# A fourth pair of row blocks in Strassen's form, in another order, in a two-layer encoder trunk

## Chip, cores and metric

One core of a Trainium2 chip runs the whole program. Time is device microseconds of that core; the figure is the median of several runs. The engines are named as the profile names them: PE (matmul; PEld is its weight load), DVE (VectorE), ACT (ScalarE), POOL (GpSimd), SP (which issues the weights' DMAs).

## The reference, cut to what matters

256 rows, width 2048, two layers, everything in float32:

```
for l in range(2):
    u = rmsnorm(x) ;  proj = u @ w_in[l]                  # latents, q/k/v, gate_a, gate_b (2048 wide each)
    y_a = mla_attention(...) @ w_o_mla[l] ;  y_b = neighbourhood_attention(...) @ w_o_na[l]
    merged = sigmoid(gate_a) * y_a + sigmoid(gate_b) * y_b
    x = x + merged @ w_out[l]
    x = x + square(relu(rmsnorm(x) @ w_ff1[l])) @ w_ff2[l]
return rmsnorm(x)
```

The change concerns the gate products (`u @` the last 4096 columns of `w_in`) and, through a shared table, `merged @ w_out`.

## The kernel before

Each float32 operand is split into a rounded high part and the low part that is left (`hi`, `lo` for weights; a `pair` holds both for an activation). A product is three matmuls: high by high, low activation by high weight, high activation by low weight. For a weight tile ACT casts the high part (L177 in `gemm_s`, L201 elsewhere) and DVE subtracts to get the low part (L178, L202).

`gemm_s` computes a product of all 256 rows with 1024 columns. It takes the 2048 rows of the weight in eight "row pairs" j of 256 rows, 1 MB each, in the sequence of a table `order`. A row pair is a 2 by 2 block product. In the plain form it has 8 block products, 24 matmuls of 512 columns; if j is in the table `pairs` it is done by a Strassen (Winograd) form with 7 products, 21 matmuls. The Strassen form needs sums: of the activation blocks, made once by DVE (L364 to L367, `sums_of`) and split by `forms` (ACT L375, DVE L376); and of the weight blocks, made for every call by DVE (L465 of 1024 columns, L468 and L469 of 512). So its weights are split from seven quarter tiles in place of four. All products of a call accumulate in eight banks of PSUM; in the end they are combined (ACT copies bank 1, L477; DVE adds, L476).

Two kinds of call concern us:

- *Gate calls*, four in each layer (`gemm_s(wi, C_GB..., ORDER, MIXED)`, then twice `C_GA`). Between the first and second stand two plain products with `w_o_na`. Their part buffers `hi` and `lo` are four each, of 1024 columns, and the sums have two buffers of 1024, one row pair's worth. The first call of a layer starts while the latents' norms (PE L329 and L298, DVE L332, L305, POOL L307, DVE L294), the rotary key (DVE L710, PE L528, DVE L530 to L532) and `forms` are still at work.
- *Output projection calls*, two in each layer (`gemm_s(w_out[l], ..., ORDER, MERGED)`). There tiles are "strips" of up to 2048 columns, three buffers each for `hi` and `lo`, and one buffer of sums.

The feed-forward calls use tables of their own (`FIRST`, `SECOND`, order 0 to 7). Tiles of 512 columns (pairs, results, forms) come from a pool of `NSLOT` slots. POOL issues the accumulating DMAs of the feed-forward (L870) and those of the bias tables; their descriptors lie in a scratch area. Weights come by SP into three `raw` buffers.

The code is recorded by a framework that orders the instructions of each engine by a timeline of its own, and gives a tile whichever buffer of its pool comes free first. Each engine then runs its instructions strictly in that order, and waits for what an instruction needs.

```
first = next(j for j in order if j in pairs)
for j in order:
    ...                       # DMA of row pair j
    if j not in pairs:  ...   # plain: cut(raw), 8 products
    if j == first: drain()    # all side work that still waits is recorded here
```

Of the kernel before, what the change touches and what calls it, by code (L numbers as in the profile page):

```python
# [58 lines left out]

NSLOT, SMALL, RBUFS, HBUFS = 52, 8, 3, 4


FIRST, SECOND = (3, 5), (2, 4, 6)


MIXED, MERGED = (1, 2, 3), (1, 2, 3)
ORDER = [0, 4, 1, 5, 2, 6, 3, 7]


SPACING, LAG1, LAG2 = 6, 13, 3
# [3 lines left out]
def trunk(ctx: ExitStack, tc: tile.TileContext, x, w_in, w_uq, w_ukv, rpb, w_o_mla, w_o_na,  # L76
# [303 lines left out]
    def blocks(acts, sums, pairs):  # L380

        def get(j):
            a = [have(acts, 2 * j + i) for i in range(2)]
            hi, lo = ([x[:, o + t * P:o + (t + 1) * P] for x in a for t in range(2)] for o in (0, S))
            if j in pairs:
                for v, x in zip((hi, lo), have(sums, j)):
                    v += [x[:, i * P:(i + 1) * P] for i in range(4)]
            return hi, lo
        return get
# [268 lines left out]
    for l in range(DEPTH):  # L658
# [57 lines left out]
        def gate(th, g):  # L716
            def evac(r):
                for i in range(2):
                    for t in range(2):
                        nc.scalar.activation(r[t, i], r[t, i], AF.Tanh, scale=mix.half[:, t:t + 1])  # L720
                        th[t, 2 * g + i] = r[t, i]
            return evac

        def local(c4):
            def merge(t, ps):
                m = part[t, c4]
                nc.vector.scalar_tensor_tensor(m, m, 1.0, ps, op0=ALU.add, op1=ALU.mult)

            gemm_a(w_o_na[l], c4 * 512, att_na, merge)

        mixed = blocks(xg, xs4, MIXED)
        gemm_s(wi, C_GB, mixed, ORDER, MIXED, gate(part, 0))
        local(0)
        local(1)
        gemm_s(wi, C_GB + 1024, mixed, ORDER, MIXED, gate(part, 1))
        for g in range(2):
            gemm_s(wi, C_GA + g * 1024, mixed, ORDER, MIXED, gate(other, g))

# [80 lines left out]
        for g in range(2):  # L819
# [10 lines left out]

            gemm_s(w_out[l], g * 1024, blocks(mg, ms4, MERGED), ORDER, MERGED, residual)
        mlp.scale()
# [126 lines left out]
```

## Time and profile before

| what | value |
|---|---|
| median of 3 runs | 2631.06 us (2629.96 to 2631.34) |
| profiled execution | 2630.92 us, span 2629.1 us |
| PE busy / DVE busy / ACT busy | 2599.1 / 2116.7 / 1457.8 us |
| granted TensorE clock | 0.998 |
| gate calls of layer 0 | 215.7 to 259.2, 281.8 to 323.3, 323.3 to 364.8, 364.8 to 406.3 us |
| output projection of layer 0 | starts at 539.4 us |

Rows of the trace read: start us, duration us, engine, line, operation, output<-inputs, shape, count, and in brackets how long the engine was idle before and what ended that. Rows of a window give for each engine the busy time in it and the count of instructions, then the granted clock, the share of the DMA engines and GB/s. Rows of waits read: who waited, for whom, us in total, times, longest. The duration of a row is longer than the distance to the next one where instructions overlap.

### The profile page before, as it was taken

Reading aid. Unit: us, or ns where it says so; the run is one execution under the profiler, and the core shown is the slowest. Engines: PE = TensorE matmul, PEld = TensorE weight load, DVE = VectorE, ACT = ScalarE, POOL = GpSimd, SP = SyncE. Lnnn points to the kernel's source line nnn. Section 1 sums busy time; section 2 is a strip of 40 time slices with the busy share of each in tenths; the row PEclk is TensorE's granted clock in tenths of the full one; section 3 lists DMA queues with packets and bytes.
Section 4 is the critical chain, followed back from the end, with each engine's and each line's share of the span. In section 5 each row is a group of like instructions: output and inputs, shape, how many; then the busy total and the mean of one; then the engine's idle time right before and its main releaser. Section 6 shows DMA issues by size and latency. Waiting matters only on the chain.

```text
span 2629.1 us, 32272 instructions
## 1 busy us (share of the span) xinstructions
PE 2599.1 (99%) x12498; PEld 2183.3 (83%) x12498; DVE 2116.7 (81%) x2496; ACT 1457.8 (55%) x1719; POOL 97.2 (4%) x117
## 2 busy tenths in 40 slices
PE   8999999999999999999999999999999999999998
PEld 7888888878888888888888888888788888888886
DVE  6678789789888888888667787896998888888885
ACT  6555556546655545546545555564566555455553
POOL 1100000000000010000001000000000000100000
PEclk9999999999999999999999999999999999999999
DMA  7555555555567485675565555644555765756744
GB/s 243 182 159 192 192 195 170 162 179 192 200 198 242 160 244 199 199 241 178 190 195 174 173 180 190 207 146 160 188 196 192 217 210 195 244 196 198 259 160 148
DMA packets 175258, 508.97 MB, mean 194 GB/s; under 512 B 13696, under 2 KB 18176, under 8 KB 175104
## 3 DMA queue, kind: packets, MB, share of 16 engines
q1 hardware_dynamic: 166192, 490.08, 55.7%
q0 software_dynamic: 8768, 16.78, 3.3%
q8 instruction: 98, 1.61, 0.2%
q14 instruction: 56, 0.46, 0.1%
q10 hardware_dynamic: 144, 0.04, 0.0%
HBM read 492.18 MB, written 2.10 MB: 188 GB/s over the span
## 4 chain that ended last, share of the span: by engine, by line
PE 76%; issue 19%; DVE 2%; ACT 1%; POOL 1%; DMA 0%; SPq 0%; POOLq 0%; DVEq 0%; ACTq 0%
PE bank L428 47%; PE bank L244 8%; PE bank L279 7%; PE bank L248 4%; PE bank L283 3%; PE bank L223 1%; PE bank L398 1%; DVE lo L178 1%; PE bank L252 1%; PE bank L224 1%; PE bank L254 1%; PE bank L253 1%; POOL xt L870 1%; PE bank L558 0%; ACT hi L177 0%
## 5 line engine op out<-in xcount | busy, mean ns | idle before, releaser
L428 PE MATMUL bank<-hi,pair 128*128 128x512 f32 x5156 | 1269.8, 390 | 7.0 <-ACT hi L177 6.2
L428 PEld LDWEIGHTS bank<-hi,pair 128*128 128x128 f32 x5156 | 964.9, 188 | 210.6 <-ACT hi L177 9.9
L177 ACT CAST hi<-raw 128x2048 fp32r<-128x2048 f32 (+3 forms) x416 | 630.0, 1534 | 449.1 <-PE bank L428 323.0
L178 DVE TENSOR_TENSOR lo<-raw,hi 128x2048 fp32r<-128x2048 f32 (+3 forms) x416 | 751.0, 1817 | 94.7 <-ACT hi L177 61.5
L428 PE MATMUL bank<-lo,pair 128*128 128x512 f32 x2578 | 677.4, 389 | 0.0
L428 PEld LDWEIGHTS bank<-lo,pair 128*128 128x128 f32 x2578 | 483.7, 188 | 100.2
L178 DVE TENSOR_TENSOR lo<-sums,hi 128x2048 fp32r<-128x2048 f32 (+1 forms) x134 | 254.6, 1909 | 176.3 <-ACT hi L177 118.5
L177 ACT CAST hi<-sums 128x2048 fp32r<-128x2048 f32 (+1 forms) x134 | 214.8, 1603 | 290.3 <-DVE sums L469 187.4
L202 DVE TENSOR_TENSOR lo<-raw,hi 128x1024 fp32r<-128x1024 f32 (+1 forms) x224 | 268.7, 1205 | 121.9 <-ACT hi L201 114.2
L201 ACT CAST hi<-raw 128x1024 fp32r<-128x1024 f32 (+1 forms) x224 | 230.0, 1036 | 208.6 <-PE bank L279 84.8
L244 PE MATMUL bank<-hi,pair 128*128 128x512 f32 x1024 | 259.6, 390 | 0.0
L244 PEld LDWEIGHTS bank<-hi,pair 128*128 128x128 f32 x1024 | 190.6, 188 | 38.9
L476 DVE TENSOR_TENSOR wide<-wide,bank 128x512 f32<-128x512 f32 x336 | 216.1, 680 | 4.5 <-PE bank L428 4.1
L279 PE MATMUL bank<-pair,hi 128*128 128x512 f32 x768 | 203.2, 397 | 4.5 <-ACT hi L201 3.2
L279 PEld LDWEIGHTS bank<-pair,hi 128*128 128x128 f32 x768 | 136.3, 190 | 26.9 <-ACT hi L201 3.6
L248 PE MATMUL bank<-lo,pair 128*128 128x512 f32 x512 | 142.8, 392 | 0.0
L465 DVE TENSOR_TENSOR sums<-raw 128x1024 f32<-128x1024 f32 x110 | 134.1, 1219 | 5.7 <-DMA raw<-in_w_ff 5.1
L283 PEld LDWEIGHTS bank<-pair,lo 128*128 128x128 f32 x768 | 106.9, 190 | 8.7
L283 PE MATMUL bank<-pair,lo 128*128 128x256 f32 x768 | 111.6, 283 | 0.0
L248 PEld LDWEIGHTS bank<-lo,pair 128*128 128x128 f32 x512 | 95.2, 188 | 18.9
L408 DVE TENSOR_TENSOR pair<-wide,pair 128x512 fp32r<-128x512 f32 x108 | 72.4, 686 | 13.9 <-ACT pair L407 13.9
L870 POOL DMA_DIRECT2D xt<-wide x48 | 42.3, 968 | 977.0 <-DVE wide L476 702.6
(131 smaller groups left out, 1727.8 us busy)
## 6 DMA issues: line engine op xcount, KB each, us to landing
raw<-in_w_ff SPq DMA_DIRECT2D x256, 1024.0 KB, 5.2
raw<-in_w_in SPq DMA_DIRECT2D x124, 1024.0 KB, 5.1
raw<-in_w_out SPq DMA_DIRECT2D x32, 1024.0 KB, 5.3
raw<-in_w_o_na SPq DMA_DIRECT2D x16, 1024.0 KB, 5.0
raw<-in_w_o_mla SPq DMA_DIRECT2D x16, 1024.0 KB, 5.0
xt<-wide POOLq DMA_DIRECT2D x48, 256.0 KB, 6.8
raw<-in_w_ukv SPq DMA_DIRECT2D x8, 1024.0 KB, 5.6
raw<-in_w_uq SPq DMA_DIRECT2D x8, 768.0 KB, 4.6
```

Of the source, the lines that this page charges most:

```text
L177: nc.scalar.copy(hi, src)
L178: nc.vector.tensor_tensor(lo, src, hi.bitcast(F32), op=ALU.subtract)
L201: nc.scalar.copy(hi, src)
L202: nc.vector.tensor_tensor(lo, src, hi.bitcast(F32), op=ALU.subtract)
L244: nc.tensor.matmul(ps[t], a, wh[:, k], start=k0 + k + i == 0, stop=False)
L248: nc.tensor.matmul(ps[t], sides(have(acts, k0 + k), t)[0], wl[:, k], start=False, stop=k0 + k == nk - 1)
L279: nc.tensor.matmul(ps[m], wh[:, k, m * P:(m + 1) * P], have(acts, k0 + k), start=k0 + k == 0, stop=False)
L283: nc.tensor.matmul(ps[m][:, :S], wl[:, k, m * P:(m + 1) * P], have(acts, k0 + k)[:, :S], start=False, stop=k0 + k == nk - 1)
L408: nc.vector.tensor_tensor(lw, src, h.bitcast(F32), op=ALU.subtract)
L428: nc.tensor.matmul(b[i], x, y, start=count[i] == 1, stop=count[i] == total[i])
L465: nc.vector.tensor_tensor(ts[0].rearrange("p (a n) -> p a n", a=2), raw[:, :512].rearrange("p (a n) -> p a n", a=1).to_broadcast([P, 2, 512]),
L476: add = lambda o, a, c: nc.vector.tensor_tensor(o, a, c, op=ALU.add)
```

## The change

```diff
-NSLOT, SMALL, RBUFS, HBUFS = 52, 8, 3, 4
+NSLOT, SMALL, RBUFS, HBUFS = 54, 8, 3, 4
...
-MIXED, MERGED = (1, 2, 3), (1, 2, 3)
-ORDER = [0, 4, 1, 5, 2, 6, 3, 7]
+MIXED, MERGED = (0, 1, 2, 3), (1, 2, 3)
+ORDER = [4, 5, 0, 1, 6, 2, 3, 7]
...
-    nc = bacc.Bacc(..., dynamic_dma_scratch_size=8192)
+    nc = bacc.Bacc(..., dynamic_dma_scratch_size=4096)
```

In the gate calls row pair 0 is done in Strassen's form too: the order was plain 0, plain 4, Strassen 1, plain 5, Strassen 2, plain 6, Strassen 3, plain 7, and is plain 4, plain 5, Strassen 0, Strassen 1, plain 6, Strassen 2, Strassen 3, plain 7. In the output projection 0 stays plain: plain 4, plain 5, plain 0, Strassen 1, plain 6, Strassen 2, Strassen 3, plain 7. The activations of pair 0 are formed once in each layer (two tiles more, hence the slots), and its activation blocks are scaled by ACT into a tile first (L501) before they are split. The halved scratch makes room for the slots. The number of DMAs is the same.

What that does to the engines' orders shows in three places. First, PE in the first gate call of layer 0, from the end of the two plain pairs; before:

```order
345 L428 MATMUL bank<-lo,pair 128x512 x8
346 L428 MATMUL bank<-hi,pair 128x512 x4
347 L428 MATMUL bank<-lo,pair 128x512 x2
348 L428 MATMUL bank<-hi,pair 128x512 x2
349 L528 MATMUL bank<-small,turn 128x256
350 L329 MATMUL bank<-ones,acc 128x2 x2
351 L428 MATMUL bank<-hi,pair 128x512 x6
352 L428 MATMUL bank<-lo,pair 128x512
353 L428 MATMUL bank<-hi,pair 128x512 x10
354 L428 MATMUL bank<-lo,pair 128x512 x4
355 L298 MATMUL bank<-diag,ones 128x128
```

and now:

```order
343 L428 MATMUL bank<-lo,pair 128x512 x8
344 L428 MATMUL bank<-hi,pair 128x512 x4
345 L428 MATMUL bank<-lo,pair 128x512 x2
346 L428 MATMUL bank<-hi,pair 128x512 x4
347 L428 MATMUL bank<-lo,pair 128x512 x2
348 L528 MATMUL bank<-small,turn 128x256
349 L329 MATMUL bank<-ones,acc 128x2 x2
350 L298 MATMUL bank<-diag,ones 128x128
351 L428 MATMUL bank<-hi,pair 128x512 x6
```

Of the matmuls ahead of L528, two high ones and a low one now belong to Strassen pair 1, not to pair 0, and the norm's L298 follows L329 with no product between them. The same stretch on DVE, now (numbers count the tiles; 2312 and 2377 are the raw weights of pairs 0 and 1):

```order
L178 TENSOR_TENSOR lo_2349<-sums_2332,hi_2348 128x1024
L323 TENSOR_TENSOR acc_2141<-acc_2141,small_2173 128x256
L260 TENSOR_TENSOR small_2225<-bank_2176,small_2223 128x256
L465 TENSOR_TENSOR sums_2379<-raw_2377 128x1024
L178 TENSOR_TENSOR lo_2385<-raw_2377,hi_2384 128x1024
L710 TENSOR_TENSOR small_2225<-small_2225,rrow_419 128x256
L468 TENSOR_TENSOR sums_2380<-raw_2377,sums_2379 128x512
L469 TENSOR_TENSOR sums_2380<-raw_2377,sums_2380 128x512
L530 TENSOR_TENSOR small_2294<-bank_2292,sin_sb_83 128x256
```

Pair 1's sums and first low part (`lo_2385`, which PE wants ahead of L528) now stand between the last part of pair 0 and the rotary key's L710, which L528 needs.

Second, ACT at the end of the third gate call; before (3277 and 3278 are the sums of pair 3, 3319 is plain pair 7):

```order
L177 CAST hi_3290<-sums_3277 128x1024
L177 CAST hi_3294<-sums_3278 128x1024
L177 CAST hi_3321<-raw_3319 128x1024
L177 CAST hi_3325<-raw_3319 128x1024
L477 COPY wide_3353<-bank_3138 128x512
```

and now (3319 and 3320 are pair 3's sums, 3361 is plain pair 7):

```order
L177 CAST hi_3332<-sums_3319 128x1024
L477 COPY wide_3395<-bank_3170 128x512
L177 CAST hi_3336<-sums_3320 128x1024
L177 CAST hi_3363<-raw_3361 128x1024
L177 CAST hi_3367<-raw_3361 128x1024
```

The copy of bank 1, which waits for PE, moved from behind pair 7's casts to ahead of pair 3's last cast.

Third, DVE in the first output projection call; before (5324 are pair 2's sums, 5387 and 5389 pair 3, 5357 plain pair 6):

```order
L178 TENSOR_TENSOR lo_5333<-sums_5324,hi_5332 128x2048
L178 TENSOR_TENSOR lo_5360<-raw_5357,hi_5359 128x2048
L170 SCALAR_TENSOR_TENSOR pair_5221<-bank_5213,pair_5221 128x256
L465 TENSOR_TENSOR sums_5389<-raw_5387 128x1024
L376 TENSOR_TENSOR pair_5238<-wide_5232,pair_5237 128x512
L468 TENSOR_TENSOR sums_5389<-raw_5387,sums_5389 128x512
L469 TENSOR_TENSOR sums_5389<-raw_5387,sums_5389 128x512
```

and now (5406 are pair 2's sums, 5439 and 5441 pair 3):

```order
L178 TENSOR_TENSOR lo_5415<-sums_5406,hi_5414 128x2048
L376 TENSOR_TENSOR pair_5290<-wide_5284,pair_5289 128x512
L178 TENSOR_TENSOR lo_5446<-raw_5439,hi_5445 128x1536
L465 TENSOR_TENSOR sums_5441<-raw_5439 128x1024
L468 TENSOR_TENSOR sums_5441<-raw_5439,sums_5441 128x512
L469 TENSOR_TENSOR sums_5441<-raw_5439,sums_5441 128x512
L178 TENSOR_TENSOR lo_5450<-sums_5441,hi_5449 128x2048
```

Plain pair 6 no longer stands between the two Strassen pairs, so no plain product's weights give time between pair 2's sums and pair 3's, which use the same buffer.

More of the change, by code (lines that the diff above doesn't have):

```diff
@@ L947 @@
                                  axis=-1).reshape(DEPTH, LORA, HEADS * (NOPE + ROPE))
-    nc = bacc.Bacc("TRN2", target_bir_lowering=False, num_devices=1, dynamic_dma_scratch_size=8192)
+    nc = bacc.Bacc("TRN2", target_bir_lowering=False, num_devices=1, dynamic_dma_scratch_size=4096)
     arrays, args = {}, []
```

## The prediction

> **What bounds the kernel now.** I read the page from its top: busy shares, the chain that ended last, then who waited on PE.
>
> ```profile
> span 2629.1 us, 32272 instructions
> PE 2599.1 (99%) x12498; PEld 2183.3 (83%) x12498; DVE 2116.7 (81%) x2496; ACT 1457.8 (55%) x1719; POOL 97.2 (4%) x117
> PE 76%; issue 19%; DVE 2%; ACT 1%; POOL 1%; DMA 0%; SPq 0%; POOLq 0%; DVEq 0%; ACTq 0%
> PE bank L428 <- ACT hi L177: 6.2, 6, 1.1
> ```
>
> PE is busy 2599.1 of 2629.1 us and the chain runs through it; in the products of `gemm_s` (L428) it waits 6.2 us in all, in six pieces. So fewer matmuls are worth their full time, as long as no new wait appears. The steady price, and what stands beside it, I take from the third gate call (323.3 to 364.8):
>
> ```profile
> 287.26 3.79 PE L428 MATMUL bank<-hi,pair 128*128 128x512 f32 x16
> ...
> 292.70 1.52 PE L428 MATMUL bank<-hi,pair 128*128 128x512 f32 x6
> ...
> 297.46 3.79 PE L428 MATMUL bank<-hi,pair 128*128 128x512 f32 x16
> ```
> ```profile
> core 0: us, PE busy (x) PEld busy (x) DVE busy (x) ACT busy (x) POOL busy (x), PEclk, DMA share, GB/s
> 323.30:364.80 41.50, 41.50 (x185) 34.37 (x184) 35.99 (x40) 24.07 (x27) 0.00 (x0) 1.00 0.58 203
> ```
> ```profile
> 333.54 2.36 DVE L178 TENSOR_TENSOR lo<-sums,hi 128x1024 fp32r<-128x1024 f32 x2 [1.90 <-PE bank L428]
> 335.82 1.22 DVE L465 TENSOR_TENSOR sums<-raw 128x1024 f32<-128x1024 f32 x1
> 336.95 1.22 DVE L178 TENSOR_TENSOR lo<-raw,hi 128x1024 fp32r<-128x1024 f32 x1
> 338.09 0.69 DVE L468 TENSOR_TENSOR sums<-raw,sums 128x512 f32<-128x512 f32 x1
> 338.69 2.36 DVE L178 TENSOR_TENSOR lo<-raw,hi 128x1024 fp32r<-128x1024 f32 x2
> 340.96 0.68 DVE L469 TENSOR_TENSOR sums<-raw,sums 128x512 f32<-128x512 f32 x1
> 341.56 0.69 DVE L178 TENSOR_TENSOR lo<-raw,hi 128x512 fp32r<-128x512 f32 x1
> 343.74 2.58 DVE L178 TENSOR_TENSOR lo<-sums,hi 128x1024 fp32r<-128x1024 f32 x2 [1.49 <-PE bank L428]
> ```
>
> A plain pair (24 matmuls) takes 292.70 − 287.26 = 5.44 us, a Strassen pair (21) 297.46 − 292.70 = 4.76, so 0.227 us a matmul. On DVE an operation starts 1.13 us after one of 1024 columns and 0.60 after one of 512. A plain pair costs DVE 2 × 1.135 = 2.27, a Strassen pair 4 × 1.135 + 3 × 0.60 = 6.34, the combination of the banks 8 × 0.60 = 4.8. Today a call needs 3 × 6.34 + 5 × 2.27 + 4.8 = 35.2 us of DVE (row: 35.99) under 41.5 of PE. DVE's idle is spent waiting for PE to give back a part buffer (1.90, 1.49): it is ahead, and that lead is the cover which the change spends.
>
> **The change, part by part.** *Saved:* eight gate calls lose 3 matmuls each, 24 × 0.227 = −5.4 us, all on the bounding engine.
>
> *Added on DVE:* 6.34 − 2.27 = 4.1 us a call; the call then needs 4 × 6.34 + 4 × 2.27 + 4.8 = 39.3 us under 41.5 − 0.7 = 40.8 of PE. It still fits, with 1.5 us left and no longer evenly: two Strassen pairs stand side by side, 12.7 us of DVE against 9.5 of PE. The duration column reads 1.22 and 0.69; that is not the pace. [...]
>
> *Steady calls (six).* Walking DVE, ACT and PE by the new order with those spacings: pair 0 is as on time as today's first Strassen pair, pair 1 gets its last high part within 0.1 us of need. Pair 3 doesn't. Its L469 ends about 22.2 us after PE began pair 0; then ACT, in order, first has the copy of bank 1, which needs pair 3's first low matmul (the 98th: 98 × 0.227, and 0.25 until the next engine starts, as from PE's fourth at 224.82 to DVE's 225.97 below: 22.5), then casts the last sums.
>
> ```profile
> 342.81 1.05 ACT L177 CAST hi<-sums 128x1024 fp32r<-128x1024 f32 x1 [0.81 <-PE bank L428]
> ...
> 357.64 0.57 ACT L477 COPY wide<-bank 128x512 f32<-128x512 f32 x1
> ```
>
> 22.5 + 0.5 + 1.05 = 24.1, where PE wants it at 102 × 0.227 = 23.15: +0.9 a call, +5.4 for six. Bounds 0 (lead kept) and 1.2 (lead gone and the copy in front).
>
> *First gate call of each layer.* Today:
>
> ```profile
> 224.82 1.98 PE L428 MATMUL bank<-lo,pair 128*128 128x512 f32 x8
> 226.64 1.07 PE L428 MATMUL bank<-hi,pair 128*128 128x512 f32 x4
> ...
> 228.46 0.59 PE L528 MATMUL bank<-small,turn 128*128 128x256 f32 x2
> 228.89 0.50 PE L329 MATMUL bank<-ones,acc 128*128 128x2 f32 x4
> ...
> 232.70 2.11 PE L428 MATMUL bank<-hi,pair 128*128 128x512 f32 x8 [1.14 <-ACT hi L177]
> ...
> 235.56 0.39 PE L298 MATMUL bank<-diag,ones 128*128 128x128 f32 x2
> ```
> ```profile
> 225.97 1.21 DVE L178 TENSOR_TENSOR lo<-sums,hi 128x1024 fp32r<-128x1024 f32 x1
> ...
> 228.57 1.22 DVE L465 TENSOR_TENSOR sums<-raw 128x1024 f32<-128x1024 f32 x1
> ...
> 230.84 0.41 DVE L530 TENSOR_TENSOR small<-bank,sin_sb 128x256 f32<-128x256 f32 x1
> 231.17 0.41 DVE L531 TENSOR_TENSOR small<-small,cos_sb 128x256 f32<-128x256 f32 x1
> ...
> 232.51 0.16 DVE L305 TENSOR_SCALAR var<-var 128x2 f32<-128x2 f32 x1
> ...
> 233.84 0.48 DVE L294 TENSOR_SCALAR diag<-ident,col 128x128 f32<-128x128 f32 x2 [0.19 <-POOL col L307]
> ```
>
> DVE has no slack here: rotary key, latent norms and forms run beside it. Before, 21 products and that wait stood between L329 and the norm's L298; in the new order L298 follows L329 at once, and a low part of pair 1 stands ahead of L528. From 228.6 on DVE: L323 and L260 (0.33 each), L465 (1.13), that low part (1.13): 231.6, where PE asked at 226.64 + 11 × 0.227 = 229.1. Then L710, L468, L469, L530, L531, L332, L532 = 0.33 + 1.2 + 0.67 + 0.07 + 0.33 = 2.6: L305 at 234.2, and L294 1.33 later (233.84 − 232.51): 235.5, so PE's L298 runs at 235.9 in place of about 230.2. PE loses 5.7, against 1.13 today: +4.6 in each layer, +9.2. The fourth pair's forms (four L364 to L367 at 0.2, L376 at 0.6) are in DVE's way before that, in gaps it now waits out. Bounds: −1.1 (today's wait goes, none comes) and +6 a layer.
>
> *Output projection (four calls).* ORDER serves these too; pairs 2 and 3, Strassen there as before, now touch, and there is one sums buffer.
>
> ```profile
> 561.89 1.91 ACT L177 CAST hi<-sums 128x2048 fp32r<-128x2048 f32 x1 [0.95 <-DVE sums L469]
> ...
> 563.84 2.29 DVE L178 TENSOR_TENSOR lo<-sums,hi 128x2048 fp32r<-128x2048 f32 x1 [0.79 <-ACT hi L177]
> ...
> 572.19 1.76 DVE L178 TENSOR_TENSOR lo<-raw,hi 128x1536 fp32r<-128x1536 f32 x1 [0.46 <-PE bank L428]
> ...
> 563.86 4.82 PE L428 MATMUL bank<-hi,pair 128*128 128x512 f32 x18 [0.82 <-ACT hi L177]
> ```
>
> From the start of pair 2's low sums to pair 3's high sums: 2.2 (to the next start, 0.08 under the duration) + 0.6 (L376) + 1.66 + 1.13 + 1.2 + 0.1 + 1.9 (cast) = 8.8 us; PE has 21 matmuls, 4.8, in between. So PE waits 4.0 less the lead with which pair 2's cast was ready. In the first call the buffer comes free 18 matmuls ahead: 4.1 − 0.26 − 1.9 = 1.9 of lead, a wait of 2.1 to 2.3, against 0.82 now: +1.5. In the second the lead is about 3.2: +0.8. Twice 2.3: +4.6. Bounds −0.8 and +3.2, and 0 and +4.0.
>
> *At nothing:* two more ACT scalings (0.4 each) of c4 = 0 in each layer: at the start ACT then waits 0.56 for the first weights (row under the clock rival), without that cover 0.8; two slots hold what the two more tiles fill; SP issues the same loads, one table a place later; the scratch, see rivals.
>
> Sum: −5.4 + 5.4 + 9.2 + 4.6 = +13.8 on the profiled execution's 2630.92 us (2629.1 span), 0.14 under the median: 2644.8.
>
> **The rivals.**
>
> *Conversion stays hidden (faster).* For it: 39.3 < 40.8. One mechanism decides: if PE finds each second adjacent pair's last high part ready, nothing above is paid and the two 1.13 us waits go: −5.4 − 2.3 = 2623. The point is a lead of 4.0 us in the output projection and 5.7 in the first gate call; the rows show 1.9 and less than none.
>
> *A wash.* Half of each wait: −5.4 + 9.6 = +4.2, 2635.
>
> *PE's clock falls after the long wait.* The wait for L298 would be 3.6 us in one piece. At the start PE idled and then:
>
> ```profile
> 9.37 3.54 PE L279 MATMUL bank<-pair,hi 128*128 128x512 f32 x8 [3.20 <-ACT hi L201]
> ...
> 8.28 1.04 ACT L201 CAST hi<-raw 128x1024 fp32r<-128x1024 f32 x1 [0.56 <-DMA raw<-in_w_in]
> ```
>
> 0.42 to 0.44 us a matmul, nearly twice 0.227. Sixteen such in each layer add 16 × 0.2 × 2 = 6.4: 2651. [...]
>
> *The halved scratch makes POOL's DMAs wait.*
>
> ```profile
> xt<-wide POOLq DMA_DIRECT2D x48, 256.0 KB, 6.8
> ```
>
> Even four in a row landing one after another take 27 us, within a projection of 82; POOL's order is unchanged and it is 4% busy. About 2645 still; 3 in 100 that it costs more.
>
> **How the numbers follow.** The measurement tells about 0.2% (5.3 us, so 2625.8 and 2636.3) from no change. Waits as worked out, whole or by more than half: 0.66; with the fallen clock: 0.09; a wash: 0.14; hidden: 0.11. Slower 0.75, same 0.14, faster 0.11. The likeliest is 2645, its own range 2637 to 2656. All low bounds give −5.4 − 2.3 − 1.6 = 2621.6, all high −5.4 + 12 + 7.2 + 14.4 = 2659. I reach down into the wash and up near the high bounds: 2629 to 2655.
>
> **What would show it.** Right: PE waits of 2 to 4 us before L528 and L298 near 229 to 236, and again in layer 2; about 0.9 in pair 3 of the other gate calls, released by ACT hi; about 2 in pair 3 of the output projection after ACT casts the sums; DVE above 90% in the gate calls. Wrong: PE waiting no more than 8 us in L428 in all (then 2623), matmuls of 0.4 us behind the long wait (2651), or POOL's DMAs landing late. The feed-forward stages should take the same time.

## The result, and the profile after

The changed kernel takes 2666.61 us (median; 2665.62 to 2668.76), the kernel before 2630.93 beside it (2629.96 to 2631.34): a ratio of 1.0138, 95% interval 1.0123 to 1.0153, or 35.7 us more. The forecast was 2645, up to 2655. The direction was right, the size was not: the rise is two and a half times the forecast's.

The page after (span and engines, then the shares of the chain that ended last):

```profile
span 2664.8 us, 32338 instructions
PE 2611.1 (98%) x12474; PEld 2184.6 (82%) x12474; DVE 2150.9 (81%) x2546; ACT 1470.9 (55%) x1741; POOL 96.5 (4%) x117
PE 73%; issue 20%; DVE 3%; ACT 2%; POOL 1%; DMA 1%; SPq 0%; DVEq 0%; POOLq 0%; ACTq 0%
```

PE has 24 matmuls fewer and is yet busy 12 us longer: somewhere the matmuls themselves became slower. PE's waits in the changed calls (who waited, for whom, us in total, times, longest):

```profile
PE bank L428 <- ACT hi L177: 21.9, 18, 3.5
PE bank L298 <- DVE diag L294: 5.0, 2, 2.6
...
PE bank L428 <- DVE lo L178: 4.8, 3, 2.3
```

Together 31.7 us, where it was 6.2. The stages' starts in the two traces tell where the 35.7 us lie (after less before, in us; a stage lasts from its first matmul to that of the next):

| stage | layer 1 | layer 2 |
|---|---|---|
| first gate call, with the two plain products behind it | +6.3 | +6.8 |
| the other three gate calls | +3.2 | +3.3 |
| MLA, up to the output projection | +0.8 | +0.8 |
| output projections, feed-forward and the rest | +7.3 | +7.7 |

Layer 1's first gate call begins 0.6 us earlier than before. The +0.8 belongs to the gate calls: in the changed kernel four products of the last gate call (0.91 us) stand behind the MLA's first matmul, L223.

PE's timeline after, layer 1: first gate call, steady gate calls, output projections (start, duration, ..., in brackets the idle time before and what ended it):

```profile
231.19 0.50 PE L428 MATMUL bank<-lo,pair 128*128 128x512 f32 x1 [2.32 <-DVE lo L178]
...
235.23 0.80 PE L298 MATMUL bank<-diag,ones 128*128 128x128 f32 x2 [2.35 <-DVE diag L294]
235.68 2.91 PE L428 MATMUL bank<-hi,pair 128*128 128x512 f32 x6
...
349.89 2.60 PE L428 MATMUL bank<-hi,pair 128*128 128x512 f32 x10 [1.02 <-ACT hi L177]
365.90 2.61 PE L428 MATMUL bank<-hi,pair 128*128 128x512 f32 x10 [0.71 <-ACT hi L177]
...
586.69 6.45 PE L428 MATMUL bank<-hi,pair 128*128 128x512 f32 x20 [2.91 <-ACT hi L177]
633.99 6.46 PE L428 MATMUL bank<-hi,pair 128*128 128x512 f32 x20 [2.02 <-ACT hi L177]
```

The six matmuls behind the wait at 235 go at about 0.45 us each, and the 20 behind the projections' waits take 6.45 us where 20 at 0.227 would take 4.5. The cause stands in the granted clock (third column from the right; after, in stretches of 3.41 us):

```profile
228.70:232.11 3.41, 1.09 (x6) 0.71 (x5) 3.38 (x6) 0.00 (x0) 0.00 (x0) 1.00 0.00 0
232.11:235.52 3.41, 1.06 (x6) 0.97 (x5) 2.91 (x10) 0.91 (x2) 0.69 (x1) 0.50 0.00 0
235.52:238.94 3.42, 3.42 (x10) 2.74 (x10) 0.25 (x1) 0.88 (x2) 0.00 (x0) 0.50 0.02 5
...
583.69:587.10 3.41, 0.50 (x3) 0.37 (x3) 1.41 (x3) 2.62 (x3) 0.00 (x0) 1.00 0.31 58
587.10:590.52 3.42, 3.42 (x10) 2.65 (x9) 3.42 (x2) 3.42 (x3) 0.00 (x0) 0.50 0.65 249
590.52:593.93 3.41, 3.41 (x17) 2.79 (x16) 2.92 (x3) 1.57 (x1) 0.00 (x0) 1.00 0.45 97
```

The clock falls to half (0.50) for one such stretch after each projection's wait and for two in each first gate call. In the kernel before, it fell only in the last 9 us of the program, and it does so still.

By cause, from these rows and the waits' totals:

| cause | us |
|---|---|
| 24 matmuls fewer, at 0.227 | −5.4 |
| waits in the first gate calls: 5.0 for L298 and 4.66 for pair 1's low part, less the 1.14 of each call before | +7.4 |
| 0.71 ahead of pair 3's last products, in all eight gate calls | +5.7 |
| 1.02 ahead of pair 1, in the third and fourth call of each layer | +4.1 |
| projections: 2.91 + 2.02, in layer 2 3.54 + 2.02, less 0.82 twice | +8.9 |
| half clock: half of PE's busy time in it, 3.41/2 = 1.7 after each of four projection waits, 2.24 in each first gate call | +11.3 |
| sum | +32.0 |

The 3.7 that are left are, for the most part, the same waits. The bracket gives the idle time between two rows, and a wait cost more than that here from start to start: in the run with the order alone (below) a gate call has one wait, of 0.71, and lasts 42.5 us for 41.5, so that it costs 1.0. Twelve waits of this kind in the gate calls, at 0.3 more each, are 3.6.

### The profile page after: what moved, and what is told of

It reads as the page before. It is cut to its first block, busy times and chain, and to the rows that moved or that the text cites. A ratio compares the mean times of both kernels' runs of the same rounds, so it can differ in the third digit from the quotient of the medians.

```text
span 2664.8 us, 32338 instructions
## 1 busy us (share of the span) xinstructions
PE 2611.1 (98%) x12474; PEld 2184.6 (82%) x12474; DVE 2150.9 (81%) x2546; ACT 1470.9 (55%) x1741; POOL 96.5 (4%) x117
## 4 chain that ended last, share of the span: by engine, by line
PE 73%; issue 20%; DVE 3%; ACT 2%; POOL 1%; DMA 1%; SPq 0%; DVEq 0%; POOLq 0%; ACTq 0%
PE bank L428 45%; PE bank L244 8%; PE bank L279 7%; PE bank L248 4%; PE bank L283 3%; ACT hi L177 1%; PE bank L223 1%; DVE lo L178 1%; PE bank L398 1%; PE bank L252 1%; PE bank L254 1%; PE bank L253 1%; PE bank L224 1%; POOL xt L870 1%; PE bank L558 0%
## 5 line engine op out<-in xcount | busy, mean ns | idle before, releaser
L428 PE MATMUL bank<-hi,pair 128*128 128x512 f32 x5140 | 1277.1, 393 | 22.2 <-ACT hi L177 21.9
L428 PEld LDWEIGHTS bank<-hi,pair 128*128 128x128 f32 x5140 | 965.9, 189 | 233.8 <-ACT hi L177 33.4
L428 PE MATMUL bank<-lo,pair 128*128 128x512 f32 x2570 | 678.0, 390 | 4.8 <-DVE lo L178 4.8
L428 PEld LDWEIGHTS bank<-lo,pair 128*128 128x128 f32 x2570 | 482.3, 188 | 106.8 <-DVE lo L178 6.9
L178 DVE TENSOR_TENSOR lo<-sums,hi 128x2048 fp32r<-128x2048 f32 (+1 forms) x150 | 274.7, 1836 | 180.0 <-ACT hi L177 146.9
L177 ACT CAST hi<-sums 128x2048 fp32r<-128x2048 f32 (+1 forms) x150 | 230.8, 1542 | 279.6 <-DVE sums L469 196.9
L202 DVE TENSOR_TENSOR lo<-raw,hi 128x1024 fp32r<-128x1024 f32 (+1 forms) x224 | 267.7, 1203 | 114.1 <-ACT hi L201 113.7
L244 PE MATMUL bank<-hi,pair 128*128 128x512 f32 x1024 | 260.7, 391 | 0.0
L244 PEld LDWEIGHTS bank<-hi,pair 128*128 128x128 f32 x1024 | 190.5, 188 | 38.3
L476 DVE TENSOR_TENSOR wide<-wide,bank 128x512 f32<-128x512 f32 x336 | 216.7, 682 | 5.5 <-PE bank L428 5.3
L465 DVE TENSOR_TENSOR sums<-raw 128x1024 f32<-128x1024 f32 x118 | 143.9, 1220 | 6.2 <-DMA raw<-in_w_ff 4.1
L469 DVE TENSOR_TENSOR sums<-raw,sums 128x512 f32<-128x512 f32 x118 | 81.0, 687 | 0.9
```

Source lines behind the costliest of these rows:

```text
L177: nc.scalar.copy(hi, src)
L178: nc.vector.tensor_tensor(lo, src, hi.bitcast(F32), op=ALU.subtract)
L202: nc.vector.tensor_tensor(lo, src, hi.bitcast(F32), op=ALU.subtract)
L244: nc.tensor.matmul(ps[t], a, wh[:, k], start=k0 + k + i == 0, stop=False)
L428: nc.tensor.matmul(b[i], x, y, start=count[i] == 1, stop=count[i] == total[i])
L465: nc.vector.tensor_tensor(ts[0].rearrange("p (a n) -> p a n", a=2), raw[:, :512].rearrange("p (a n) -> p a n", a=1).to_broadcast([P, 2, 512]),
```

## The experiments

Theory A, held first: neighbouring Strassen pairs, and a first gate call in which no products cover the side work, make PE wait, and the clock falls behind the long waits. Against it stood: the room made for it (slots, scratch), DVE's load in whatever order, and matmuls slow for other reasons than the clock.

**Slots and scratch alone.**

```diff
-NSLOT = 52; dynamic_dma_scratch_size=8192
+NSLOT = 54; dynamic_dma_scratch_size=4096
```

> The kernel before with the change's 54 slots and halved DMA scratch, nothing else; every engine's order stays as before. Theory A (the loss is PE waits in the gate and projection calls, and a clock that falls behind the long ones): room costs nothing, 2631 us within 2. Rival (the scratch makes POOL's DMAs late, or the other addresses of the tiles cost something): 2641 or more, some of it in the feed-forward stages.

Measured: 2630.62 us beside 2630.91, ratio 1.0000 (0.9991 to 1.0009). The room costs nothing; that term of the prediction holds.

**Gates alone, and projections alone.**

```diff
 (the changed kernel)
-gemm_s(w_out[l], ..., ORDER, MERGED, residual)
+gemm_s(w_out[l], ..., [0, 4, 1, 5, 2, 6, 3, 7], MERGED, residual)
 (the kernel before)
-gemm_s(w_out[l], ..., ORDER, MERGED, residual)
+gemm_s(w_out[l], ..., [4, 5, 0, 1, 6, 2, 3, 7], MERGED, residual)
```

> The changed kernel, but the two output projections of each layer take their row pairs in the old order again. Theory A, from the stages of the trace after: per layer the first gate call lost about 6.5 us, the three others 3.2, the stage behind them 1.0; twice 10.7 is +21, so about 2652 us. By the prediction's own terms for the gates (-5.4 + 5.4 + 9.2) it would be 2640. If the gate calls as such are innocent and the projection alone costs: 2626 to 2631.

> The kernel before, but the two output projections of each layer take their row pairs in the new order; gates, slots and scratch as before. Theory A, from the stages of the trace after: +7.5 us in each layer (waits of about 2.9 and 2.0 us ahead of pair 3, and half the clock for some 3.4 us behind each), so 2646. By the prediction's term (+4.6 in all): 2636. If the projection is innocent: 2631. Together with the run before it the differences should add up to the whole change, +35.7; if they do not, the two parts act on each other.

Measured: the gates alone 2652.67, +21.8 (1.0069 to 1.0096); the projections alone 2643.62, +12.7 (1.0034 to 1.0059). Together 34.5 of 35.7: the two parts are separate, and each is more than twice what the prediction gave it (+9.2 and +4.6). The timeline of the projections alone:

```profile
577.13 6.45 PE L428 MATMUL bank<-hi,pair 128*128 128x512 f32 x20 [2.95 <-ACT hi L177]
...
624.43 6.44 PE L428 MATMUL bank<-hi,pair 128*128 128x512 f32 x20 [2.02 <-ACT hi L177]
...
1886.78 4.85 PE L428 MATMUL bank<-hi,pair 128*128 128x512 f32 x20 [2.82 <-ACT hi L177]
```

The third row is the surprise: a wait of 2.82 with no slow matmuls behind it (20 in 4.85), though 2.02 was enough elsewhere. So the length of a wait alone does not decide the clock.

**The order alone, without the fourth pair.**

```diff
-MIXED, MERGED = (0, 1, 2, 3), (1, 2, 3)
+MIXED, MERGED = (1, 2, 3), (1, 2, 3)
```

> The changed kernel with the new order everywhere, but row pair 0 plain in the gate calls as before: order alone, no fourth Strassen pair. Theory A (neighbouring Strassen pairs cause the waits): pairs 2 and 3 touch still, 0 and 1 do not; +15 of the projection, +0.9 in each of six gate calls, the first gate calls about as before, so about 2651. Rival B (the order alone does it): the cost of the change plus the saving it loses, 2667 + 5 = 2672. Rival C (only the DVE load of the fourth pair costs in the gates): 2646.

Measured: 2652.52, +21.6 (1.0068 to 1.0093), as theory A has it. In its trace 11.8 of it are the projections with the feed-forward, 4.4 the steady gate calls, 2.0 the first ones (44.6 us each for 43.6), 2.1 the stage behind the gates, where 0.91 in each layer are again products of the last gate call behind L223. So the new order costs about 8.2 us in the gates without any fourth pair: pair 3's wait of 0.71 stands in each of the eight calls, and its rows in layer 1's steady calls (318.40, 360.91, 403.42) lie 42.51 us apart.

```profile
318.40 2.59 PE L428 MATMUL bank<-hi,pair 128*128 128x512 f32 x10 [0.71 <-ACT hi L177]
...
403.42 2.59 PE L428 MATMUL bank<-hi,pair 128*128 128x512 f32 x10 [0.71 <-ACT hi L177]
```

What the fourth pair adds lies mostly in the first gate calls (50 us for 44.6).

**The fourth pair in the old order.**

```diff
-ORDER = [4, 5, 0, 1, 6, 2, 3, 7]
+ORDER = [0, 4, 1, 5, 2, 6, 3, 7]
```

and the same with three pairs in the first gate call of each layer:

```diff
+gemm_s(wi, C_GB, mixed, ORDER, (1, 2, 3), gate(part, 0))
```

> The changed kernel with the four Strassen pairs kept, but the old order 0 4 1 5 2 6 3 7 everywhere: in the gate calls a plain pair stands behind each Strassen pair, and the projections run as before. Theory A (neighbouring Strassen pairs overload DVE for a stretch; over a whole call it has room, 39.3 of 40.8 us): the six steady gate calls gain their 0.68 each, -4.1; the first gate call of a layer, where pair 0 now comes at once and DVE still has the side work, lies between -0.7 and +4 each; 2626 to 2635 us. Rival D (four Strassen pairs are too much for DVE in whatever order): the gates lose as they did in the kernel with the change's gates alone, less what the order alone cost there (2 x 4.3): 2644 or more.

> As the kernel before it in this list (old order, four Strassen pairs), but the first gate call of each layer keeps three Strassen pairs, so that only the six steady calls have four. Theory A: the first calls as in the kernel before, six times -0.68: 2627 us. If the lead that DVE brings from call to call is used up: within 2 of 2631. Rival D: 2637 or more (a wait of about 1 us in each of six calls, beyond the saving).

Measured: 2652.82, +22.4 (1.0071 to 1.0099), a miss; and 2631.69 beside 2630.41, ratio 1.0005 (0.9996 to 1.0014). The whole loss of the first run is its first gate calls. With pair 0 first, all side work is recorded at the start of the call, with no products between (and the clock stays at half for three stretches, 219.8 to 230.1):

```profile
224.02 1.01 PE L329 MATMUL bank<-ones,acc 128*128 128x2 f32 x4 [7.12 <-DVE acc L323]
226.67 0.77 PE L298 MATMUL bank<-diag,ones 128*128 128x128 f32 x2 [1.64 <-DVE diag L294]
```

The second run gains next to nothing in its six steady calls although no Strassen pairs touch there any more: three calls are 0.3 us shorter in each layer, of 2.0 saved, and the first gate call, beside which pair 0's activations are still formed, is 0.4 longer. Its three steady calls of layer 1 (windows; the fifth column is DVE) and the starts of the last two:

```profile
282.00:406.30 124.30, 123.49 (x542) 101.13 (x541) 114.12 (x127) 73.81 (x84) 0.00 (x0) 1.00 0.58 193
```
```profile
330.22 0.73 PE L428 MATMUL bank<-lo,pair 128*128 128x512 f32 x2 [0.41 <-DVE lo L178]
...
372.01 0.73 PE L428 MATMUL bank<-lo,pair 128*128 128x512 f32 x2 [0.40 <-DVE lo L178]
```

DVE is busy 114.1 of 124.3 us, 92%. In the last two calls PE loses about 0.8 where pair 0's low part is late, which takes back the 0.68 saved in the call.

**Filling the projection's waits.** Nine matmuls of a zero weight, ahead of pair 3's first product with sums:

```diff
 (on the projections alone)
+for _ in range(9): matmul(b[3], zero, mg[0], start=False, stop=False)
```

> The kernel with the new order in the projections alone (2643.6 us), and in each of the four projection calls nine more matmuls of a zero weight, 2.04 us, at the place where PE waits for pair 3's sums, so that PE works in most of that wait; they add zero to a bank (DMA scratch halved, to have room for the zeros). Theory A (part of the loss is the halved clock behind the wait): the waits last as before but are filled, no clock falls near 577, 625 and 1933, and three times 1.7 us come back: 2638.5. Rival E (the clock has no part in it; matmuls behind the wait are slow because weights or DMAs crowd them): no gain, 2643.6, or up to 2652 if the nine matmuls are paid in full.

Measured: 2645.92, 2.3 more than without them: a miss in the sum, and the most telling run. First and second projection call of layer 1:

```profile
572.77 2.27 PE L432 MATMUL bank<-pair,zero 128*128 128x512 f32 x9
...
576.41 4.86 PE L428 MATMUL bank<-hi,pair 128*128 128x512 f32 x20 [0.67 <-ACT hi L177]
...
618.36 2.27 PE L432 MATMUL bank<-pair,zero 128*128 128x512 f32 x9
...
624.26 6.46 PE L428 MATMUL bank<-hi,pair 128*128 128x512 f32 x20 [2.01 <-ACT hi L177]
```

In the first call theory A holds: the wait was filled, the clock stayed up, 20 matmuls take 4.86 again. In the second call PE came 2 us later and waited 2.01 as before, so this wait does not end at a time that DVE sets; it follows PE. ACT's timeline of that call in the changed kernel shows why:

```profile
631.55 0.59 ACT L477 COPY wide<-bank 128x512 f32<-128x512 f32 x1 [3.96 <-PE bank L428]
632.03 1.90 ACT L177 CAST hi<-sums 128x2048 fp32r<-128x2048 f32 x1
```

ACT, in order, first has the copy of bank 1, which needs one of PE's last three matmuls before the wait (from 631.13), and only then the cast that PE waits for: 0.5 + 1.9 us, however early the sums are. (Their last part, DVE L469, ended at 631.0.) The two second calls thus paid their nine matmuls in full (+4.1), and one fall less gave 1.7 back: +2.4.

**When the clock falls.** No encoder: 48 stretches of matmuls with gaps between.

```
for k, n in enumerate(gaps):                       # n: 0 to 47, in mixed order
    matmul(bank, g[:, :128], a, start=True, ...)   # waits for the cast into g
    90 to 130 more matmuls into the same bank
    ACT: bank -> src (scaled by 0) ; cast src[:, :128+64*n] -> g
```

> No encoder at all: 48 stretches of 91 to 131 matmuls of 512 columns, with a gap of PE between them that grows with one ACT cast of 128 to 3136 columns (gaps of about 0.7 to 4 us, at all phases). It shows which gaps make the granted clock fall. Theory A1 (the clock is decided at the ends of a running window of 3.41 us, by whether PE was idle in more than about half of it): gaps under 1.7 us never, over 3.4 always, those between by where they lie in the window; each fall lasts one window. Rival A2 (a threshold on the gap alone, about 2 us): all above it fall, none below, whatever the phase. Rival A3 (only gaps over 3.4 us): none below.

47 gaps of 0.71 to 3.21 us lie between stretches; the clock fell after 16 of them, the shortest 1.98, and not after a gap of 2.94. All falls lie on one grid of 3.413 us, within 0.01 us. At the end of each stretch of that grid in which PE idled 1.89 us or more the clock fell; up to 1.88 it never did (the two nearest lie less than 0.01 apart, which is how well edges and starts are known). Three gaps, of 2.89, 2.94 and 1.98 us (windows; second column the length, third PE, and the granted clock third from the right):

```profile
171.77:175.18 3.41, 1.46 (x7) 0.88 (x5) 0.00 (x0) 1.82 (x2) 0.00 (x0) 1.00 0.00 0
175.18:178.59 3.41, 2.47 (x6) 1.99 (x7) 0.00 (x0) 0.88 (x1) 0.00 (x0) 0.50 0.00 0
178.59:182.01 3.42, 3.42 (x10) 2.65 (x9) 0.00 (x0) 0.00 (x0) 0.00 (x0) 0.50 0.00 0
536.99:540.41 3.42, 1.53 (x7) 0.94 (x5) 0.00 (x0) 1.76 (x2) 0.00 (x0) 1.00 0.01 2
540.41:543.82 3.41, 2.36 (x10) 1.96 (x11) 0.00 (x0) 1.00 (x1) 0.00 (x0) 1.00 0.00 0
...
711.07:714.49 3.42, 1.44 (x6) 0.87 (x6) 0.00 (x0) 1.80 (x2) 0.00 (x0) 1.00 0.02 5
714.49:717.90 3.41, 3.41 (x9) 2.63 (x8) 0.00 (x0) 0.00 (x0) 0.00 (x0) 0.50 0.00 0
```

The gap of 2.94 falls across an edge, 1.88 on one side and 1.06 on the other, and nothing happens; 1.98 within one stretch was enough. Behind a rest of 0.94 idle in the halved stretch (second row) the clock stayed down for one more. So where the gap lay decided, as theory A1 has it; A2 and A3 fall. The changed kernel's six falls inside the program lie on such a grid too (232.11, 587.10 and so on, 104, 118, 387, 491 and 505 times 3.413 from the first), and the wait of 2.82 that brought no fall in the run of the projections alone was cut by an edge into 1.25 and 1.57:

```profile
1881.80:1885.21 3.41, 2.16 (x10) 1.46 (x8) 2.93 (x4) 0.97 (x2) 0.00 (x0) 1.00 0.00 0
1885.21:1888.63 3.42, 1.85 (x8) 1.46 (x9) 1.87 (x1) 3.42 (x3) 0.00 (x0) 1.00 0.81 220
```

In the runs of the encoder, too, behind their start, no stretch at full clock with up to 1.72 us idle brought a fall (but for one, with 1.42, under strict alternation below), and after each with 1.91 or more it came.

**The copy behind the cast.** One zero matmul more into bank 1, with pair 3's last high sums, in each gate and projection call:

```diff
 products((1, ...), ..., (4, a22, l22, *w4))
+if j == 3: mm(1, zero, w4[0])      # L477's copy now needs the cast of w4
```

> The changed kernel, but in the gate and projection calls bank 1 gets one more matmul, of a zero weight with pair 3's last high sums. So the copy of bank 1 (ACT L477) can't be ready before the cast of those sums, and it moves behind it in ACT's order; 12 matmuls more, +2.7 us. Theory F (the copy, which waits for PE, stands in front of a cast that PE waits for: this is the wait of 0.71 in each gate call's pair 3 and the 2.02 in the second projection call): seven or eight waits of 0.71 go, the 2.02 falls to about 1.0 (the sums are ready 1 us earlier), and the two clock falls behind it go: -5.7 - 2.0 - 3.4 + 2.7 = about -8, 2658 us; the 2.9 of the first projection call stays. Rival G (DVE makes the sums too late, the copy in front costs nothing): 2667 to 2669.

Measured: 2660.58, ratio to before 1.0112 (1.0098 to 1.0126): 6.0 less than the changed kernel by the medians, 8 expected. Its steady gate calls (the waits ahead of pair 1) and layer 1's projections:

```profile
349.56 2.60 PE L428 MATMUL bank<-hi,pair 128*128 128x512 f32 x10 [0.85 <-ACT hi L177]
392.15 2.61 PE L428 MATMUL bank<-hi,pair 128*128 128x512 f32 x10 [0.86 <-ACT hi L177]
...
584.83 3.78 PE L428 MATMUL bank<-hi,pair 128*128 128x512 f32 x8 [2.84 <-ACT hi L177]
632.66 2.11 PE L428 MATMUL bank<-hi,pair 128*128 128x512 f32 x8 [1.09 <-ACT hi L177]
```

All waits of 0.71 in the steady calls are gone (0.05 is left, once 0.18), and in layer 1 the 2.02 is 1.09, with no fall behind it: theory F. The 0.85 ahead of pair 1 and the first projection's 2.84 stay: there ACT waits for DVE's sums. In layer 2 the second projection still waits 1.91 with a fall; its cast begins at 1947.33, right behind DVE's L469 (1946.53), so there the sums are late and the copy is not what PE waits for. And behind layer 1's first projection wait the clock now stays at half for two stretches (584.11 to 590.94) where it was one. By stages the gates gave back 5.3 us and the projections, with the feed-forward, 1.5 (the first gate call begins 0.7 later).

**A plain pair between 0 and 1 in the first gate call.**

```diff
-gemm_s(wi, C_GB, mixed, ORDER, MIXED, gate(part, 0))
+gemm_s(wi, C_GB, mixed, [4, 5, 0, 6, 1, 7, 2, 3], MIXED, gate(part, 0))
```

> The changed kernel, but the first gate call of each layer takes its pairs in the order 4 5 0 6 1 7 2 3: still four Strassen pairs, but a plain pair between 0 and 1, so that PE has products between the latent norm's L329 and L298 again and no low part of pair 1 stands ahead of L528. Theory A: the two waits (2.32 and 2.35) and the two halved windows (3.4 us lost) of that call go, of 6.5 us in each layer some 5 to 7 come back: 2653 to 2657 us. Rival D (DVE has too much to do there with four pairs and the side work, in any order): the waits only move, 2663 or more.

Measured: 2655.45 (1.0080 to 1.0107 of before), 11.2 less than the changed kernel. The first gate calls take 44.7 us for 49.9, and no clock falls in them. PE's only waits there, in layer 1:

```profile
231.62 0.67 PE L528 MATMUL bank<-small,turn 128*128 128x256 f32 x2 [1.35 <-issue]
...
258.75 1.20 PE L428 MATMUL bank<-hi,pair 128*128 128x512 f32 x4 [0.71 <-ACT hi L177]
```

So it was not DVE's load (the fourth pair is still there) but the place of pair 1's first low part and of the norm's L298.

**Strict alternation, plain pair first.**

```diff
 (projections old, first gate call with three pairs in the old order)
-ORDER = [4, 5, 0, 1, 6, 2, 3, 7]
+ORDER = [4, 0, 5, 1, 6, 2, 7, 3]
```

> Four Strassen pairs in the six steady gate calls, strictly alternating and beginning with a plain pair (4 0 5 1 6 2 7 3); the first gate call of each layer with three pairs and the projections as in the kernel before. In the run with 0 4 1 5 2 6 3 7 the third and fourth call of a layer lost 0.84 us each where pair 0's low part was late at the start of the call. Theory A: with a plain pair ahead that wait goes, all of -4.1 shows: 2627 us. Rival H (the call now ends with a Strassen pair, all eight banks end at once and PE waits for the first four to be read): some 1 to 2 us a call more, 2633 to 2639.

Measured: 2639.29, +8.3 (1.0019 to 1.0043): rival H, at the upper end of what it said. With a Strassen pair last, all banks end together, and the next call's products wait for the sums that read them:

```profile
328.07 1.21 PE L428 MATMUL bank<-hi,pair 128*128 128x512 f32 x4 [0.93 <-DVE wide L476]
```

Some 1.6 us of it are something else. In layer 2's first gate call the clock falls once, behind a stretch with only 1.42 us idle (the third row is back at 1.00):

```profile
1536.69:1540.10 3.41, 1.99 (x11) 1.64 (x11) 3.38 (x7) 1.04 (x1) 0.00 (x0) 1.00 0.03 5
1540.10:1543.51 3.41, 3.41 (x10) 2.65 (x9) 1.86 (x8) 0.91 (x2) 0.69 (x1) 0.50 0.00 0
1543.51:1546.93 3.42, 3.42 (x18) 2.86 (x18) 2.43 (x3) 2.44 (x3) 0.00 (x0) 1.00 0.23 29
```

Two matmuls of 256 columns (L528) and four of 2 (L329) stand in that stretch. In the run above, the same stretch with 1.39 us idle (1543.10 to 1546.51) brought no fall. So 1.89 is the figure of a run with matmuls of 512 columns alone; why less is enough here was not tested.

**All causes out at once, and a second buffer of sums.**

```diff
 (the changed kernel: first gate call 4 5 0 6 1 7 2 3, zero matmul in the gate calls, projections in the old order)
 (the projections alone)
-whole_ts = spool.tile([P, 2048], F32, tag="sums", bufs=1)
+whole_ts = spool.tile([P, 2048], F32, tag="sums2" if pairs is MERGED and j == 3 else "sums", bufs=1)
```

> All the named causes taken out of the changed kernel at once, with its four Strassen pairs kept in all eight gate calls: the first gate call of each layer in the order 4 5 0 6 1 7 2 3, a zero matmul in the gate calls that moves the copy behind the cast (8 of them, +1.8 us), the projections in the old order. If the causes are separate: 2655.5 (first call mended) - 13.3 (projections, between 12.7 and 13.9 by the two runs that separate them) - 4.3 (six waits of 0.71) + 1.8 = 2639.7 us, and no clock falls before the end. If the causes hang together (time given back at one place is lost at the next, because DVE has no lead): 2645 or more. What would be left above the kernel before: four waits of 0.86 ahead of pair 1 (3.4), the zeros (1.8), about 1 in each first call.

> The kernel with the new order in the projections alone (2643.6 us), but pair 3's weight sums get a buffer of their own there (DMA scratch halved, to make room), so that DVE can make them before it subtracts pair 2's low sums; in the order that follows the copy of bank 1 also stands behind pair 3's cast. The prediction's step (one sums buffer, DVE's chain from pair 2's low sums to pair 3's cast) and theory F (the copy in front) both say that the waits of 2.9 and 2.0 nearly go, and with them the falls of the clock: 2631 to 2634. If DVE's throughput with two Strassen pairs side by side is the limit, whatever the buffers: the waits stay over 1 us, 2638 or more.

Measured: 2641.95 (1.0029 to 1.0056) where separate causes gave 2639.7, so 24.7 of the 35.7 us are accounted for by removal; no clock falls before the end. Its waits in L428 for ACT are 8.1 us in all, 0.85 ahead of pair 1 among them. The zero matmul brings a wait that neither part had: behind each first gate call PE waits 1.3 us for the copy (L244 for ACT L477, 2.7 in all), about what is missing.

And 2635.39 (1.0011 to 1.0028): with a buffer of its own for pair 3's sums, in the same neighbouring order, the projections' waits shrink to

```profile
570.36 3.28 PE L428 MATMUL bank<-hi,pair 128*128 128x512 f32 x13 [0.65 <-ACT hi L177]
...
615.00 3.48 PE L428 MATMUL bank<-hi,pair 128*128 128x512 f32 x14 [0.94 <-ACT hi L177]
```

and no clock falls before the end: 8.2 of the 12.7 us come back. Both waits now stand ahead of pair 2; ahead of pair 3 none is left. The copy has also moved behind pair 3's cast here (575.95 for 572.11), so this run takes out both causes; the copy alone, above, left the first call's 2.84. The larger part of the projections' loss was thus one buffer and the copy in front, not DVE's throughput. Of the 4.8 us that stay, 1.7 are a longer wait where the projections begin (1.99 for 1.13 in each layer); the rest was not traced. No version beat the kernel before.

## Why the prediction was wrong, point by point

- *Saved, −5.4, and start, slots, scratch at nothing:* right.
- *First gate calls, +9.2:* the mechanism was right and the size nearly: pair 1's low part made PE go on at 231.2 (231.6 foretold), L298 ran at 235.2 (235.9). The waits cost +7.4; the run with a plain pair between took them away. What was left out is the pair 3 wait in these calls and the clock.
- *Steady calls, +5.4:* the copy L477 in front of pair 3's last cast is what was foretold, 0.71 for 0.9, in eight calls. That "pair 1 gets its last high part within 0.1 us of need" failed: 1.02 in the third and fourth call of each layer (+4.1). In the second call DVE stands idle 2.25 and 3.61 us waiting for PE, and pair 1 is in time. In the third it works from 324.9 to 337.8 without a gap, with the eight L476 of the call before among its own work, and has no lead left at pair 1. The walk of the prediction was of a call that starts with a lead; that the L476 are what used it up is read from the order, not tested. Besides, the wait of 0.71 cost 0.3 more than its bracket, which the price left out.
- *Output projections, +4.6:* they cost 12.7. The chain through the one buffer of sums is the mechanism of the first call (2.91, 3.54 in layer 2, for 2.1 to 2.3). In the second call the step failed in kind: in layer 1 the lead was nearly there (1.09 of wait once the copy was out of the way, for 0.8), but the copy in front of the cast, which I had seen in the gate calls, made it 2.02. In layer 2 the wait with the copy moved is 1.91, by DVE's sums.
- *The clock, a rival at 9%, held to one place:* this step cost the forecast. The sum has no term for the clock; as a rival it was priced for L298's wait alone, 16 matmuls in each layer, for a wait of 3.6 us in one piece. No run shows the 16, and the matmuls of 0.42 to 0.44 us at the start, which the rival was read from, ran at a granted clock of 1.00 (before, 9.37 to 12.75 us). In the changed kernel the first gate calls lost 2.24 us each to the half clock, for the 3.2 of that sum, and the clock fell at six places, behind waits of 2.02 to 3.54. In the gap run, 1.89 us idle in a stretch of 3.41 was enough: +11.3, a third of the whole loss. The waits that made it fall were foretold at 2.1 to 2.3 in the first projection call; by the gap run those are long enough where no edge cuts them. The sign that the prediction gave for this rival came: 0.45 us a matmul behind L298's wait.
- *Hidden, wash:* the changed kernel was neither. The run with the old order and four pairs in the six steady calls alone is a wash, 0.05% from before: with DVE busy 92% of the time, PE loses in new waits nearly all that it saves.

The parts of the error: 11.3 clock + 4.3 projection waits + 4.4 gate waits ahead of pairs 1 and 3 − 1.8 first calls + 3.7, for the most part what waits cost beyond their brackets, = 21.9 us. The clock's part is worked out from half of PE's busy time at half clock; where one fall was taken away (first projection call, nine zero matmuls) 20 matmuls took 1.6 us less.

## What to carry to other kernels

An engine that still fits over a whole call (39.3 of 40.8 us) can already be the bound in the order that the call is served in: walk two calls in a row, not one, and look for an operation that waits for the bounding engine and stands, in order, ahead of one that this engine waits for. Price a PE wait of 2 us as up to 3.7, as here, where the half clock behind a wait of 2.02 cost an estimated 1.7 more (half of 3.41), and a short wait as more than its bracket: the one of 0.71 cost 1.0. A buffer more (8 KB a partition here), with the order that followed from it, took away most of what two neighbouring Strassen pairs cost in the projections.

## What the runs showed of the hardware

In the gap run, with matmuls of 512 columns, the granted clock fell from 1.00 to 0.50 at the edge of a grid of 3.413 us when PE had idled 1.89 us or more in the stretch that ended there (1.88: no fall; 47 gaps), and stayed there for 3.41 us, or for two such stretches (175.18 to 182.01). By the encoder's rows a stretch at 0.50 with PE busy throughout cost an estimated 1.7 us, half its length; a gap from 1.98 to 2.94 us cost that beyond its length, or nothing, by where it lay, so the same wait had two prices: in the run with a plain pair between 0 and 1, layer 1's second projection wait of 2.02 (630.04) brought no fall, layer 2's (1944.76) did.

```profile
630.04 4.83 PE L428 MATMUL bank<-hi,pair 128*128 128x512 f32 x20 [2.02 <-ACT hi L177]
...
1944.76 6.44 PE L428 MATMUL bank<-hi,pair 128*128 128x512 f32 x20 [2.02 <-ACT hi L177]
```

Behind one stretch with small matmuls in it the clock fell at 1.42 us idle.
